# Gate modulation products of two blocks in one chained run, with four raw weight tiles and two tiles for each weight part

## The chip, the cores and the metric

The kernel runs on one core of a Trainium2 chip. The time is that of the device in microseconds (us), the median of the runs shown; one further execution was taken by the hardware profiler, and everything said of single instructions comes from it. The engines are called PE (matrix products; PEld is its loading of weights), DVE (vector), ACT (scalar and activation), POOL and SP (which issues the transfers).

## The reference

One step of a hybrid backbone: 128 context tokens and 512 latent tokens, model width 1024. Everything is float32.

```python
shift, scale, gate = jnp.split(mod, 3, axis=-1)      # mod = silu(c) @ w_ada + b_ada
h = _rmsnorm(x, g_pre) * (1 + scale) + shift
proj = h @ w_in                                      # 3840 columns
qa, ka, va, ga, qr, zf, zb, ir, gr, uf, gf = _split_columns(proj)
oa  = neighbourhood / context attention of (qa, ka, va)          # 8 heads x 64
o_r = bidirectional gated linear recurrence of (qr, zf, zb, ir)  # 4 heads, normed
o_f = Fourier mixing of uf, then a linear map
mixed = concat([oa * silu(ga), o_r * silu(gr), o_f * silu(gf)])
out = mixed @ w_out
x = x + gate * _rmsnorm(out, g_post)
```

The last third of `w_ada`, 1024 x 1024, makes `gate`, once for the context vector and once for the latent one. These products are what the change regroups.

## The kernel before

**Weights.** A block is 128 columns of `w_in` (BLOCKS, L24), a tile of 128 partitions by 1024 values, 512 KB. `load_raw` (L172) loads it into a tile tagged "raw"; all such loads are kept in program order on SP's queue. `split_w` (L178) makes two parts of it: `hi`, a rounded copy (a cast on ACT, L127), and `lo`, the remainder (a subtraction on DVE, L128). A product is three matmuls: hi with the high part of h, hi with its low part, lo with the high part (`mm3`, L208). The high and low parts of the modulated h stand in `hT[0]` and `hT[1]`. The dictionary WB (L27) says how many tiles a tag has: two "raw", three "hi", three "lo", eight "pT" of the same size, and so on. A tile is given again when all that read it is done, and whoever wants it waits until then.

**Start.** `start_stream` (L242) makes the modulated h in eight slices k = 0 to 7. For each slice `mod_cols` (L192) forms shift and scale for 128 columns with narrow matmuls: the stationary operand is 128 x 32 (`csil`), four of them side by side write four groups of 32 partitions, and each of the 8 float32 products becomes two instructions, so 16 for each block of 128 columns. Here two blocks (shift and scale) go into one PSUM tile one after the other. `zf_stream` (L281) follows slice by slice with the first two blocks, zf0 and zf1, whose parts are held until k = 7 is done: 2 blocks x 2 halves of the tokens x 8 slices x 3 matmuls of 320 columns. `fill` (L956) starts with "h4" and takes the other blocks in the order of FILL (L30); the first is zb0, whose first half goes along with the slices that are there. Two blocks of `ir` are held at once (`token_blocks`, L348).

**Middle.** The recurrence (L414) and the attention (L637) run beside the blocks as generators; a small planner, `Order` (L39), interleaves them in the program by estimated times. The tile framework then schedules the instructions with a timeline of its own, in which an instruction that is earlier in the program goes first when it is ready, and gives the tiles. What stands is an order for each engine that is fixed before the run.

**The gate.** `gate_vectors` (L844) waits for blocks WG = 18 onward. At each of eight blocks it loads 128 columns of `wg` into a "raw" tile, takes a PSUM tile with tag "f", runs `mod_cols` into it, and splits the 128 x 128 result into one half of two `row` tiles. After every second block, four matmuls with `selr` spread the rows over the partitions, and DVE adds the bias and multiplies by `g_post`. PSUM has eight tiles: five with tag "b", three with "f"; the accumulators of the blocks, the Fourier stage and the gate all use "f".

**End.** FILL ends with gf0, gf1, the two Fourier blocks uf0 and uf1, F0 (the Fourier stage joins the streams), ga2 and ga3. Then `out_first` (L895) computes the first 512 columns of the output projection and `out_second` (L919) the rest. `out_units` (L885) loads the four weight tiles kk in the order 2, 0, 1, 3 through "raw" and splits them into "hi" and "lo", or into two "pT" tiles for the kk that are named in `late`. The products run over k in the order 4, 5, 0, 1, 6, 7, 2, 3 (`kord`), where kk = k // 2, each in one accumulator; their moving operand is `w`, the stationary one `mh`, the split of the mixed branches.

`follow` (L115) is a helper that ties an instruction behind the last one of a list, as an order on the same engine; the recurrence and the attention scores use it.

Of the kernel before, what the change touches and what calls it, by code (L numbers as in the profile page):

```python
# [10 lines left out]
F32R = mybir.dt.float32r  # L11
# [6 lines left out]
P = 128  # L18
# [5 lines left out]
BLOCKS = ["zf0", "zf1", "zb0", "qr0", "zb1", "qr1", "ir0", "ir1", "gr0", "gr1", "va0", "qa0", "ka0", "ga0", "gf0", "va1",  # L24
          "qa1", "ka1", "ga1", "gf1", "va2", "qa2", "ka2", "ga2", "ga3", "va3", "qa3", "ka3", "uf0", "uf1"]
TOKENS = ("ir",)
WB = {"raw": 2, "hi": 3, "lo": 3, "t": 18, "pe": 2, "o": 4, "cf": 3, "pb": 5, "pf": 3, "s": 8, "m": 4, "row": 2, "tbl": 1, "pT": 8, "vs": 2, "kc": 4}  # L27
RAW = ["vs", "pT", "pT", "pT"] * 4
EARLY = 3
FILL = "zb0 qr0 zb1 qr1 ir0 P0 P1 ga0 P2 gr0 gr1 ga1 P3 gf0 gf1 uf0 F0 ga2 ga3"  # L30
# [41 lines left out]
def mixer_kernel(ctx: ExitStack, tc: tile.TileContext, A, O):  # L72
# [5 lines left out]
    wp = ctx.enter_context(tc.tile_pool(name="wp", bufs=1))  # L78
    tp = ctx.enter_context(tc.tile_pool(name="tp", bufs=WB["t"]))
    sp = ctx.enter_context(tc.tile_pool(name="sp", bufs=WB["s"]))  # L80
    ps = ctx.enter_context(tc.tile_pool(name="ps", bufs=8, space=PSUM))

    od = Order()
# [3 lines left out]
    def nm(s):  # L87
        n_[0] += 1
        return f"{s}_{n_[0]}"

    def T(cols=NT, dt=F32, tag=""):
        return tp.tile([P, NT], dt, tag="t", name=nm("t" + tag))[:, :cols]

    def PE_():
        return tp.tile([P, 512], F32, tag="pe", name=nm("pe"), bufs=WB["pe"])

    def S(cols):
        if cols <= 16:
            return sp.tile([P, 16], F32, tag="s", name=nm("s"))[:, :cols]
        return sp.tile([P, 320], F32, tag="m", name=nm("m"), bufs=WB["m"])[:, :cols]  # L100

    def C():
        return sp.tile([P, 256], F32, tag="cf", name=nm("cf"), bufs=WB["cf"])

    def PB(tag="b"):
        return ps.tile([P, 512], F32, tag=tag, name=nm("pb"), bufs=WB["p" + tag])

    last_tr = [None]

    def mm(out, lhsT, rhs, start=True, stop=True):  # L110
        n, m = rhs.free_size(), lhsT.free_size()
        od.now += 1e-3 * (n * 0.4167 * 4 if rhs.dtype == F32 else max(n * 0.4167, m * 0.83)) + 2e-3
        return te.matmul(out, lhsT, rhs, start=start, stop=stop).ins  # L113

    def follow(chain, ins):  # L115

        if chain:
            tc.add_manual_dep(ins, chain[-1].name, mybir.DependencyInfo(mybir.DependencyClass.NoSync,
                                                                        mybir.DependencyReason.DATA), reason="turns")
        chain.append(ins)  # L120
# [5 lines left out]
    def split(src, hi, lo, hi_eng=None, lo_eng=None):  # L126
        (sc.copy if hi_eng is None else hi_eng.tensor_copy)(hi, src)  # L127
        (ve if lo_eng is None else lo_eng).tensor_sub(lo, src, hi.bitcast(F32))  # L128
# [5 lines left out]
    def const(name, shape, dt=F32, dma=gp.dma_start):  # L134
        t = cp.tile([P, *shape], dt, tag=name, name=name)
        if name in A:
            dma(t, A[name])
        return t
# [27 lines left out]
    csil = const("csil", [KT, 32])  # L166
# [5 lines left out]
    def load_raw(src, tag, shape=(KT, P)):  # L172
        t = (tp if tag == "vs" else wp).tile([P, *shape], F32, tag=tag, name=nm(tag), bufs=WB[tag])
        with tc.issue_after(wdma[-1]) if wdma else ExitStack():
            wdma.append(sy.dma_start(t, src).ins)
        return t
# [6 lines left out]
    def load_w(src, lo_eng=None, shape=(KT, P), tags=("raw", "hi", "lo")):  # L183

        return split_w(load_raw(src, tags[0], shape), lo_eng, shape, tags[1:])

    def load(t, src):

        with tc.issue_after(wdma[-1]) if wdma else ExitStack():
            sy.dma_start(t, src)  # L190

    def mod_cols(out, w):  # L192

        t = od.now
        for k in range(KT):
            o = out[32 * (k % 4):32 * (k % 4) + 32, :]
            mm(o, csil[:, k, :], w[:, k, :], start=(k < 4), stop=(k >= 4))
        od.now = t + 0.45

    shift, G, rstd = const("shift", [KT, 2]), const("G", [KT, 2]), const("rstd", [5])  # L200
# [643 lines left out]
    def gate_vectors():  # L844
        selr = cp.tile([P, 2, P], F32R, tag="selr", name="selr")
        gp.tensor_copy(selr, sel)
        for q in range(8):
            yield f"block{WG + q}"
            hf = q // 4
            w = load_raw(A["wg"][q], "raw")  # L850
            if q % 4 == 0:
                gbias = T(512), T(512)
                for t, name in zip(gbias, ("bgate", "gpost")):
                    load(t, A[name][hf * 512:hf * 512 + 512].partition_broadcast(P))
                if True:
                    if q == 0:
                        gc = sp.tile([P, 2, 512], F32, tag="masks", name="gc", bufs=1)
                    gg[0][hf], gg[1][hf] = gc[:, hf, :], T(512)
                else:
                    gg[0][hf], gg[1][hf] = T(512), T(512)  # L860
            if q % 2 == 0:
                rows = [sp.tile([P, 256], F32R, tag="AC", name=nm("row"), bufs=2) for _ in range(2)]
            pm, es = PB("f"), slice(q % 2 * P, q % 2 * P + P)
            mod_cols(pm[:, 0:P], w)
            split(pm[:, 0:P], *[t[:, es] for t in rows])
            if q % 2 == 0:
                continue
            yield 1.0
            pg, cs = PB("f"), slice(q % 4 * P - P, q % 4 * P + P)
            for d in range(2):  # L870
                for a in range(2):
                    mm(pg[:, d * 256:d * 256 + 256], selr[:, d, :], rows[a], start=(a == 0), stop=(a == 1))
            for d in range(2):
                g = gg[d][hf][:, cs]
                ve.tensor_add(g, pg[:, d * 256:d * 256 + 256], gbias[0][:, cs])
                ve.tensor_mul(g, g, gbias[1][:, cs])
# [4 lines left out]
    def out_mm(po, w, i, k, first, last):  # L881
        for a, (pw, hh) in enumerate(((0, 0), (0, 1), (1, 0))):
            mm(po, mh[k][hh][:, i * P:(i + 1) * P], w[pw], start=(first and a == 0), stop=(last and a == 2))

    def out_units(hf, late):  # L885
        units = {}
        for kk in (2, 0, 1, 3):
            w = load_w(A["wout"][hf, kk], shape=(2, 512), tags=("raw", "pT", "pT") if kk in late else ("raw", "hi", "lo"))
            for j in range(2):
                units[2 * kk + j] = (w[0][:, j, :], w[1][:, j, :])  # L890
        return units
# [3 lines left out]
    def out_first():  # L895
        for k in kord[:2]:
            t = tp.tile([P, 2, NT], F32R, tag="vs", name=nm("mh"), bufs=WB["vs"])
            mh[k] = [t[:, j, :] for j in range(2)]
        mh[kord[2]] = [tp.tile([P, NT], F32R, tag="o", name=nm("mh"), bufs=WB["o"]) for _ in range(2)]
        rest = [big.tile([P, KT, NT], F32R, tag=f"hT{j}", name=f"mh{j}") for j in range(2)]  # L900
        for k in kord[3:]:
            mh[k] = [t[:, k, :] for t in rest]
        units = out_units(0, (3,))
        banks = [PB() for _ in range(4)]
        for n, k in enumerate(kord):
            yield f"m{k}"
            split(mx[k], *mh[k])
            yield 1.8
            for i in range(4):
                out_mm(banks[i], units[k], i, k, n == 0, n == KT - 1)  # L910
                yield 0
        banks.append(PB("b" if WB["pb"] > 4 else "f"))
        for n, k in enumerate(kord):
            out_mm(banks[4], units[k], 4, k, n == 0, n == KT - 1)
        for i in range(5):
            pos[i][0] = banks[i]
        yield 0
# [38 lines left out]
    def fill():  # L956
        yield "h4"
        for step in FILL.split():
            if step == "|":
                yield 0  # L960
                continue
            n, p = step[:2], int(step[-1])
            if n == "zb":
                yield from block(step, lambda z, u: gate(p, 1, z, u), ve)
            elif n == "qr":
                yield from block(step, lambda z, u: query(p, z, u), ve)
            elif n == "ir":
                yield from value_blocks()
            elif n[0] == "P":
                yield from attention_blocks(p)  # L970
            elif n[0] == "m":
                yield step
            elif n == "uf":
                yield from fourier_blocks()
            elif n == "F0":
                od.streams.insert(0, [fourier(), od.now])
            else:
                yield from gate_block(step)
        yield from out_first()
        yield from out_second()  # L980
# [7 lines left out]
    od.add(recurrence(1))  # L988
    od.add(attentions())
    od.add(gate_vectors())  # L990
    od.add(fill())
    od.run()
# [136 lines left out]
```

## Time and profile before

| | us |
|---|---|
| median of 3 runs | 436.22 (436.12 to 437.0) |
| profiled execution | 437.11 |
| its span | 435.3 |
| PE busy | 411.3 (94% of the span) |
| PE weight loads busy | 372.7 |
| DVE busy | 303.5 |
| ACT busy | 205.8 |

The span runs from the first instruction to the last. Busy times of PE are modelled from pipelined instructions, so that two that overlap both show their full duration; what one costs is read from the distance to the start of the next. Rows of the timeline give start, duration, engine, line, operation, the names of what is written and read, and how often it follows itself. A bracket at a row's end gives the idle time ahead of it and what ended it. A line is often that of a helper (L113 is every matmul, L127 and L128 every split), so the names of the tiles tell what it is: `raw,csil` are the gate's narrow matmuls, `hT,hi` and `hT,lo` those of the blocks, `hi,hT` those of ir, `hi,mh` and `pT,mh` those of the output projection, `t,t` those of the recurrence and of the Fourier stage.

### The profile page before, as it was taken

How to read it: one execution, taken by the hardware profiler on the slowest of the kernel's cores; microseconds unless marked ns; L12 is line 12 of the kernel's file. 1: busy time of each engine (PE TensorE's matmuls, PEld its weight loads, DVE VectorE, ACT ScalarE, POOL GpSimd, SP SyncE). 2: the span in 40 equal slices, each digit the busy share in tenths (PEclk: the TensorE clock that was granted, in tenths of full speed). 3: DMA queues.
4: the chain of work that ended last, by engine and by line, in shares of the span. 5: the costliest groups of instructions: out<-in, count | busy, mean ns of one | idle time of the engine just before them, and what ended most of it. 6: DMA issues, size and time to landing. Idle time of an engine off the chain costs nothing.

```text
span 435.3 us, 8309 instructions
## 1 busy us (share of the span) xinstructions
PE 411.3 (94%) x3176; PEld 372.7 (86%) x3176; DVE 303.5 (70%) x866; ACT 205.8 (47%) x546; POOL 7.4 (2%) x23
## 2 busy tenths in 40 slices
PE   0699999999998999999999999999999999999994
PEld 0488899999988998999899889889898988988884
DVE  2775479999986866885597658885768928670174
ACT  6434467565341526654444444753556643350161
POOL 2000000000020100000000000000000000000000
PEclk9999999999999999999999999999999999999998
DMA  7996153211302021122021413245134302481023
GB/s 236 412 407 229 49 158 114 74 45 50 88 20 76 10 62 48 56 97 74 32 68 60 145 50 104 98 147 163 51 119 150 96 0 66 140 291 48 0 105 139
DMA packets 19528, 47.62 MB, mean 109 GB/s; under 512 B 3184, under 2 KB 6912, under 8 KB 19488
## 3 DMA queue, kind: packets, MB, share of 16 engines
q1 hardware_dynamic: 19376, 46.94, 32.0%
q8 instruction: 25, 0.41, 0.4%
q0 software_dynamic: 112, 0.14, 0.3%
q14 instruction: 15, 0.12, 0.1%
HBM read 43.80 MB, written 3.28 MB: 108 GB/s over the span
## 4 chain that ended last, share of the span: by engine, by line
PE 90%; DVE 3%; DMA 3%; ACT 1%; issue 1%; SPq 0%; DVEq 0%; ACTq 0%
PE pb L113 84%; PE pb L124 7%; DMA vs<-wss 2%; DMA txa<-x 1%; DVE AL L450 1%; DVE t L524 1%; DVE AL L487 0%; ACT L679 0%; DVE t L951 0%; ACT pe L680 0%; DVE t L467 0%; DVE t L466 0%; DVE AC L450 0%; DVE t L468 0%; SPq L190 0%
## 5 line engine op out<-in xcount | busy, mean ns | idle before, releaser
L113 PE MATMUL pb<-hT,hi 128*128 128x320 f32 x896 | 208.7, 317 | 2.5 <-DVE vs L128 1.5
L113 PEld LDWEIGHTS pb<-hT,hi 128*128 128x128 f32 x896 | 148.7, 188 | 9.0 <-issue 3.3
L113 PE MATMUL pb<-hT,lo 128*128 128x320 f32 x448 | 139.1, 312 | 0.0
L113 PEld LDWEIGHTS pb<-hT,lo 128*128 128x128 f32 x448 | 84.0, 188 | 1.3 <-DVE G L272 0.2
L128 DVE TENSOR_TENSOR lo<-raw,hi 128x1024 fp32r<-128x1024 f32 x35 | 42.8, 1223 | 18.7 <-ACT hi L127 18.5
L127 ACT CAST hi<-raw 128x1024 fp32r<-128x1024 f32 x35 | 36.8, 1050 | 28.4 <-PE pb L113 17.5
L113 PE MATMUL pb<-t,t 64*128 64x128 f32 (+2 forms) x414 | 42.9, 291 | 0.4 <-DVE AL L450 0.4
L113 PEld LDWEIGHTS pb<-t,t 64*128 64x128 f32 (+1 forms) x414 | 36.0, 188 | 4.7 <-issue 0.7
L127 ACT CAST pT<-pb 128x256 fp32r<-128x256 f32 x64 | 23.5, 373 | 22.3 <-DVE pT L128 11.1
L113 PE MATMUL pb<-hi,mh 128*128 128x512 f32 (+1 forms) x108 | 30.8, 375 | 0.0
L128 DVE TENSOR_TENSOR pT<-pb,pT 128x256 fp32r<-128x256 f32 x64 | 26.5, 419 | 1.7 <-ACT pT L127 1.5
L679 ACT ACTIVATE pe<-pb,s 128x256 f32<-128x256 f32 x32 | 15.3, 478 | 17.5 <-DVE s L678 8.4
L113 PEld LDWEIGHTS pb<-hi,mh 128*128 128x128 f32 x108 | 19.6, 188 | 3.7 <-DVE mh L128 0.3
L113 PE MATMUL pb<-pT,mh 128*128 128x512 f32 (+1 forms) x102 | 21.9, 364 | 0.0
L124 PE MATMUL pb<-ident,pe 128*128 128x128 f32 x136 | 21.0, 274 | 0.5 <-ACT pe L680 0.5
L113 PEld LDWEIGHTS pb<-pT,mh 128*128 128x128 f32 x102 | 17.7, 189 | 3.1
L113 PE MATMUL pb<-lo,mh 128*128 128x512 f32 (+1 forms) x54 | 19.5, 375 | 0.0
L934 ACT ACTIVATE t<-pb 128x512 f32<-128x512 f32 (+1 forms) x11 | 6.1, 552 | 26.9 <-PE pb L113 26.7
L690 DVE TENSOR_TENSOR o<-pb,o 64x512 f32<-64x512 f32 (+1 forms) x16 | 7.8, 486 | 15.5 <-ACT o L689 15.4
L124 PEld LDWEIGHTS pb<-ident,pe 128*128 128x128 f32 x136 | 16.5, 140 | 1.7 <-ACT pe L680 0.7
L450 DVE COPY_PREDICATED AL<-masks,pb 128x512 f32<-128x512 uint32 x24 | 16.6, 742 | 1.7 <-PE pb L113 1.6
L113 PE MATMUL pb<-pT,vs 128*128 128x256 f32 (+1 forms) x96 | 17.0, 320 | 0.0
(205 smaller groups left out, 635.3 us busy)
## 6 DMA issues: line engine op xcount, KB each, us to landing
raw<-win SPq DMA_DIRECT2D x30, 512.0 KB, 3.5
pT<-wss SPq DMA_DIRECT2D x12, 512.0 KB, 10.3
raw<-wg SPq DMA_DIRECT2D x8, 512.0 KB, 3.6
raw<-wout SPq DMA_DIRECT2D x8, 512.0 KB, 3.6
t<-x SPq DMA_DIRECT2D x10, 256.0 KB, 5.4
o_y<-t SPq DMA_DIRECT2D x9, 256.0 KB, 2.2
vs<-wss SPq DMA_DIRECT2D x4, 512.0 KB, 9.5
tbl<-tbl SPq DMA_DIRECT2D x4, 512.0 KB, 3.5
```

Of the source, the lines that this page charges most:

```text
L113: return te.matmul(out, lhsT, rhs, start=start, stop=stop).ins
L124: last_tr[0] = te.transpose(out, src, ident).ins
L127: (sc.copy if hi_eng is None else hi_eng.tensor_copy)(hi, src)
L128: (ve if lo_eng is None else lo_eng).tensor_sub(lo, src, hi.bitcast(F32))
L450: ve.copy_predicated(out, mk.to_broadcast([P, i1 - i0, P]), src)
L524: ve.scalar_tensor_tensor(sall[r, cdst], sall[r, cs], Td[r, ip:ip + 1], pst[r, cdst], op0=ALU.mult, op1=ALU.add)
L679: sc.activation(pe[:, 256:512], ss[:, 256:512], ACT.Exp, bias=m[:, 1:2], accum_out=m[:, 3:4])
L690: ve.tensor_add(out, src[r, :], out)
L934: sc.activation(T(512)[:, cs], po[:, 0:cs.stop - cs.start], ACT.Square, accum_out=ssb[:, j:j + 1])
```

## The change

`mod_cols` ties its instructions behind one another through a list that the caller can hand on. `gate_vectors` loads nothing at an even block; at the odd one it loads both weights, runs the 32 instructions of the two in one chain into one PSUM tile of 256 columns, and splits 256 columns at once. The tag "raw" has four tiles, "hi" and "lo" two each. Since `out_units` has two pairs of "hi" and "lo", kk = 1 of the first half goes to "pT" along with kk = 3.

```diff
-WB = {"raw": 2, "hi": 3, "lo": 3, "t": 18, ...
+WB = {"raw": 4, "hi": 2, "lo": 2, "t": 18, ...
...
-    def mod_cols(out, w):
-
-        t = od.now
+    def mod_cols(out, w, chain=None):
+
+        t, chain = od.now, [] if chain is None else chain
         for k in range(KT):
             o = out[32 * (k % 4):32 * (k % 4) + 32, :]
-            mm(o, csil[:, k, :], w[:, k, :], start=(k < 4), stop=(k >= 4))
+            follow(chain, mm(o, csil[:, k, :], w[:, k, :], start=(k < 4), stop=(k >= 4)))
         od.now = t + 0.45
...
         for q in range(8):
             yield f"block{WG + q}"
             hf = q // 4
-            w = load_raw(A["wg"][q], "raw")
+            chain = []
             if q % 4 == 0:
...
             if q % 2 == 0:
-                rows = [sp.tile([P, 256], F32R, tag="AC", name=nm("row"), bufs=2) for _ in range(2)]
-            pm, es = PB("f"), slice(q % 2 * P, q % 2 * P + P)
-            mod_cols(pm[:, 0:P], w)
-            split(pm[:, 0:P], *[t[:, es] for t in rows])
-            if q % 2 == 0:
                 continue
+
+            rows = [sp.tile([P, 256], F32R, tag="AC", name=nm("row"), bufs=2) for _ in range(2)]
+            pm = PB("f")
+            for u, ww in enumerate([load_raw(A["wg"][q - 1 + j], "raw") for j in range(2)]):
+                mod_cols(pm[:, u * P:(u + 1) * P], ww, chain)
+            split(pm[:, 0:256], *rows)
             yield 1.0
...
-        units = out_units(0, (3,))
+        units = out_units(0, (1, 3))
```

`mod_cols` of the start stage is called without a chain, so that each of its calls ties its own 16 instructions.

More of the change, by code (lines that the diff above doesn't have):

```diff
@@ L26 @@
 TOKENS = ("ir",)
-WB = {"raw": 2, "hi": 3, "lo": 3, "t": 18, "pe": 2, "o": 4, "cf": 3, "pb": 5, "pf": 3, "s": 8, "m": 4, "row": 2, "tbl": 1, "pT": 8, "vs": 2, "kc": 4}
+WB = {"raw": 4, "hi": 2, "lo": 2, "t": 18, "pe": 2, "o": 4, "cf": 3, "pb": 5, "pf": 3, "s": 8, "m": 4, "row": 2, "tbl": 1, "pT": 8, "vs": 2, "kc": 4}
 RAW = ["vs", "pT", "pT", "pT"] * 4
```

## The prediction

> **What bounds the kernel now.** I read the page first (busy shares, then the chain of work that ended last), then the stretches view, whose columns are stretch, length, and each engine's busy time with its count.
>
> ```profile
> span 435.3 us, 8309 instructions
> ...
> PE 411.3 (94%) x3176; PEld 372.7 (86%) x3176; DVE 303.5 (70%) x866; ACT 205.8 (47%) x546; POOL 7.4 (2%) x23
> ...
> PE 90%; DVE 3%; DMA 3%; ACT 1%; issue 1%; SPq 0%; DVEq 0%; ACTq 0%
> ```
> ```profile
> core 0: us, PE busy (x) PEld busy (x) DVE busy (x) ACT busy (x) POOL busy (x), PEclk, DMA share, GB/s
> 54.00:134.00 80.00, 78.17 (x678) 73.37 (x678) 73.87 (x179) 45.13 (x107) 2.42 (x6) 1.00 0.24 75
> 134.00:385.00 251.00, 250.53 (x1850) 230.03 (x1851) 177.90 (x546) 121.74 (x362) 1.91 (x6) 1.00 0.27 86
> ```
>
> The chain is 90% PE. PE rests 80.00-78.17 = 1.83 us between 54 and 134 and 0.47 in the 251 us after that. So two things count: work taken off PE is a gain almost one for one, and a hole opened in PE is a loss almost one for one, because no later rest exists to swallow it. A deeper prefetch of raw weights (four tiles for two) has no hole to close between 134 and 385. The change makes PE's work smaller (the gate's runs) and thins the cover that keeps PE fed (two slots for a weight's parts where three stood).
>
> **Part 1, the gate's runs.** One gate block issues 16 of the narrow 128x32 instructions, eight blocks 128. Rows of the timeline of PE (start, duration), and one piece of the chain in order of time:
>
> ```profile
> 34.26 1.01 PE pb L113 x32
> ```
> ```profile
> 245.25 0.42 PE L113 MATMUL pb<-raw,csil 128*32 128x128 f32 x6
> 245.60 0.66 PE L124 MATMUL pb<-ident,pe 128*128 128x128 f32 x4
> ...
> 270.51 0.31 PE L113 MATMUL pb<-hT,lo 128*128 128x320 f32 x1
> 270.75 0.64 PE L113 MATMUL pb<-raw,csil 128*32 128x128 f32 x16
> 271.33 0.56 PE L113 MATMUL pb<-hT,hi 128*128 128x320 f32 x2
> ...
> 330.10 0.64 PE L113 MATMUL pb<-raw,csil 128*32 128x128 f32 x14
> ```
> ```profile
> 53.90:57.60 3.70, 3.65 (x25) 3.65 (x26) 0.00 (x0) 1.00 0.17 24
> ```
>
> In the timeline, what PE pays is the distance to the next row's start. A run of 16 takes 271.33-270.75 = 0.58 us; the chain's piece of 32, from the first stage, has the same instructions of two blocks in 1.01. The difference, 0.43 for 16, is 0.027 us an instruction, which leaves 0.15 a run whatever its length. Entering costs more: 270.75-270.51 = 0.24, where a 320-column matmul otherwise takes 3.65/25 = 0.147 (last row, the stretches view of the matmuls on hT). I put leaving at 0.10, an estimate of the size of entering (0.09). A run's fixed price is 0.15+0.09+0.10 = 0.34 us. From the first row (245.25) to the last (330.10) the timeline has thirteen runs: the eight blocks are cut five times, as by the transposes at 245.60. The added chain orders the 32 instructions of a pair among themselves; it keeps no others out. Bounds: four clean runs, 9 x 0.34 = **-3.1 us**; ten runs, if cuts come per instruction, **-1.0**. I take seven: 6 x 0.34 = **-2.0**.
>
> The work around them, from the views of the tiles row and raw and the page's list of DMA issues:
>
> ```profile
> L127 ACT CAST row<-pb x8: 266/268/283, 246.9 to 332.5; 128x128 fp32r<-128x128 f32 x8
> L128 DVE TENSOR_TENSOR row<-pb,row x8: 280/287/292, 247.4 to 332.8; 128x128 fp32r<-128x128 f32 x8
> ```
> ```profile
> L175 SPq DMA_DIRECT2D raw<-wg x8: 327/328/372, 204.9 to 314.6; - x8
> ```
> ```profile
> raw<-wg SPq DMA_DIRECT2D x8, 512.0 KB, 3.6
> ```
>
> Eight evictions on each engine become four of twice the width: between nothing and half of 8 x 0.28, a gain of 1.1 us on ACT and on DVE, behind a PE without a rest, so nothing. The eight gate loads stay eight; the even one is issued at the odd one's turn, on SP behind the loads of one more block. The first now stands 40 us ahead of its matmuls and the last 15 (314.6 to 330.1): nothing, and one landing of 3.6 us were the lead all gone. Four raw tiles hold a pair and leave two to the blocks between.
>
> **Part 2, two slots, at the start.** Both zf blocks keep their slots until the last modulated tile, k = 7. Today zb0 takes the third; rows of ACT, of DVE, of the stretches view for matmuls on hT, and of PE:
>
> ```profile
> 42.29 1.04 ACT L127 CAST hi<-raw 128x1024 fp32r<-128x1024 f32 x1
> ...
> 51.84 1.28 ACT L323 ACT_TABLE_LOAD   x1 [2.22 <-PE pb L113]
> 53.13 0.44 ACT L323 ACTIVATE t<-pb 128x320 f32<-128x320 f32 x1
> ```
> ```profile
> 44.23 1.22 DVE L128 TENSOR_TENSOR lo<-raw,hi 128x1024 fp32r<-128x1024 f32 x1
> ...
> 50.18 0.83 DVE L239 TENSOR_TENSOR hT<-t,hT 128x640 fp32r<-128x640 f32 x1
> ```
> ```profile
> 22.00:53.90 31.90, 20.52 (x120) 17.78 (x120) 10.02 (x15) 1.00 0.60 231
> ```
> ```profile
> 53.95 0.56 PE L113 MATMUL pb<-hT,hi 128*128 128x320 f32 x2 [1.02 <-ACT t L324]
> ```
>
> 120 matmuls on hT ran by 53.9; zf owns 2x2x8x3 = 96, so 24 are zb0's first half: 24 x 0.147 = 3.5 us that fill PE while it waits for k = 6 and 7. They can't run there any more. In return the subtraction at 44.23 (1.22 us) leaves DVE and those 24 leave PE's queue ahead of k = 7, whose tile I therefore put at 49.6 instead of 51.0. zf's first block then ends its 6 matmuls at 50.3; cast (1.04), subtraction (1.22) and two handovers of 0.1, an estimate, make zb0 ready at 52.8. If ACT takes the table load and a sigmoid first, as at 51.84 now, it is 1.7 later. PE then owes 46 matmuls where it owes 24 at 53.95 today: the loss is that time + 22 x 0.147 - 53.95, so 2.1 to 3.8, and 1.4 if k = 7 gains another 0.7. I take **+2.8**, the table load half avoided. Nothing else fills the hole: all other work needs zf, or a block behind zb0 in the same slots.
>
> **Middle.** A block lasts 48 x 0.147 = 7 us and its parts are ready some 2.5 us after a slot comes free, so one block ahead is enough, save for ir, which holds two pairs at once:
>
> ```profile
> 82.41 1.05 ACT L127 CAST hi<-raw 128x1024 fp32r<-128x1024 f32 x1 [1.98 <-PE pb L113]
> ...
> 101.77 1.05 ACT L127 CAST hi<-raw 128x1024 fp32r<-128x1024 f32 x1
> ```
> ```profile
> 83.84 1.39 PE L113 MATMUL pb<-t,t 64*128 64x128 f32 x20
> 85.15 0.50 PE L113 MATMUL pb<-hi,hT 128*128 128x256 f32 x2
> ...
> 104.38 0.45 PE L113 MATMUL pb<-hT,hi 128*128 128x320 f32 x2
> ```
>
> These casts run as qr1's slot and ir's first come free; after the change they serve ir's second part and va0, ready 2.5 us on, at 84.9 and 104.3. PE wants them at 85.15 (the recurrence's 20 run before) and 104.38. Nothing to 1.5 us: **+0.2**.
>
> **End.** In each accumulator the output projection's unit kk = 2 comes first. Today its cast takes the third slot at 341.26; rows of ACT and DVE, then the stretches view for matmuls on mh (the projection's) and for those on hT:
>
> ```profile
> 341.26 1.04 ACT L127 CAST hi<-raw 128x1024 fp32r<-128x1024 f32 x1 [0.17 <-PE pb L113]
> ...
> 364.83 1.05 ACT L127 CAST hi<-raw 128x1024 fp32r<-128x1024 f32 x1
> ```
> ```profile
> 367.66 1.22 DVE L128 TENSOR_TENSOR lo<-raw,hi 128x1024 fp32r<-128x1024 f32 x1
> ```
> ```profile
> 357.30:361.00 3.70, 2.20 (x9) 1.57 (x9) 0.00 (x0) 0.00 (x0) 1.00 0.00 0
> 364.70:373.30 8.60, 8.32 (x35) 6.32 (x35) 0.82 (x1) 0.07 (x1) 1.00 0.22 63
> ```
> ```profile
> 344.30:348.00 3.70, 3.65 (x24) 3.52 (x24) 0.00 (x0) 1.00 0.51 148
> 348.00:361.00 13.00, 0.12 (x1) 0.18 (x1) 0.00 (x0) 1.00 0.00 0
> 361.00:364.80 3.80, 3.75 (x24) 3.42 (x24) 0.00 (x0) 1.00 0.53 172
> ```
>
> The two hT rows with 24 are ga2's halves. With two slots ga2 and ga3 hold both, and kk = 2 waits for ga2's end at 364.8: the cast at 364.83 becomes its own, the subtraction ends at 368.9 (as now, behind Fourier's additions) or at 367.1 (DVE free at once). Gone are the 9 matmuls before 361, 2.1 us, and those from 365.2 until then: 1.9 to 3.7 us of hole. If the Fourier matmuls behind the 9 move up, they take the first 2.1 back. So 1.9 to 5.8; I take **+3.7**, moved up and DVE as busy as now. kk = 1 in pT costs the same cast and subtraction; kk = 0 waits for kk = 2's release, covered by ga3's 48 matmuls (7 us), and by nothing if ga3 runs early (2.5).
>
> **Sum.** -2.0+2.8+0.2+3.7 = +4.7 us. The profiled execution took 437.11 (its span 435.3, 1.8 around it), so 441.8; it stood 0.9 above the median of 436.22, on which it is **440.9**. The terms' ends: -3.1+1.4+0+1.9 = +0.2 (436.4) and -1.0+3.8+1.5+5.8 = +10.1 (446.3).
>
> **Rivals.**
> *Two slots are enough (faster).* PE's order is planned anew. If ga2's second 24 matmuls follow its first at 348 instead of 361, the slot is free 13 us sooner and kk = 2 is ready in time; the point that decides is ga2 ending 2.5 us before 357.3. Then the end costs nothing, and with the start at 1.4 and clean runs at -3.1 the sum is -1.7: 434.5 (433.1 with no hole at the start). For it: one block's length separates them, and nothing they multiply is late. Against it: PE passed them over for 13 us while it took the lower-ranked projection, so a PSUM bank held them, and that stays. [...]
> *The hole slows the clock (slower).* The stretches view at the end of the span, after PE's last matmul:
>
> ```profile
> 429.50:431.50 2.00, 0.00 (x0) 0.00 (x0) 1.54 (x4) 0.69 (x3) 0.00 (x0) 1.00 0.00 0
> 431.50:433.50 2.00, 0.00 (x0) 0.00 (x0) 0.50 (x2) 0.00 (x0) 0.00 (x0) 0.57 0.72 254
> ```
>
> The granted clock falls some 2 us after PE stops. [...] Against: the hole may be split in two. [...]
> *The runs stay cut (slower).* Twelve in place of thirteen: -0.3, and the sum is +6.4: 442.6. For it: five cuts in eight short groups.
>
> **Chances.** Forecast 0.55, enough slots 0.21, clock 0.12, cut runs 0.12. About 0.2% (0.9 us) is what a measurement here can tell from no change; the forecast's low end and weaker forms of the first rival give 0.08 to that: slower 0.73, same 0.08, faster 0.19. The range for 8 in 10 is 434.2 to 445.5; the forecast's own is 436.4 to 446.3.
>
> **What would show it.** About seven narrow runs after 240 us; zb0's cast behind zf's last matmul and a rest of PE of 2 us or more near 51; the projection's first matmul behind ga2's last, with rests near 357 or 365; PE's rests up by some 6 us. No rest near 365, or ga2's matmuls in one piece, would make it wrong.

## The result and the profile after

| | before | after |
|---|---|---|
| median, us (runs) | 436.31 (436.12 to 437.0, 4 runs) | 443.59 (443.14 to 443.88, 4 runs) |
| profiled execution, us | 437.11 | 443.88 |
| its span, us | 435.3 | 442.1 |

The ratio is 1.0163 with a 95% interval of 1.0145 to 1.0181: slower by 7.3 us, where the forecast had 4.7 us. An execution over 1.5% above the fastest of its kernel counts as slow and is in no median, interval or ratio of this document; that concerns two of four of the pairing alone and one of four of kk = 2 elsewhere. First the page of the profile after: the span, part 1 and the chain of work that ended last.

```profile
span 442.1 us, 8316 instructions
...
PE 413.4 (93%) x3176; PEld 374.5 (85%) x3176; DVE 303.5 (69%) x862; ACT 203.6 (46%) x542; POOL 7.4 (2%) x23
...
PE 86%; DVE 5%; DMA 4%; ACT 3%; issue 1%; SPq 1%; DVEq 0%; ACTq 0%
```

PE fell from 90% of the chain to 86%, and DVE, DMA and ACT rose: work that had been beside PE stands on the path now. The stretches view of the same two stretches that the prediction shows (columns as there) says where.

```profile
54.00:134.00 80.00, 79.62 (x673) 75.29 (x673) 69.30 (x164) 41.34 (x101) 2.42 (x6) 0.98 0.23 78
134.00:385.00 251.00, 247.38 (x1840) 227.40 (x1839) 180.65 (x556) 121.00 (x359) 1.91 (x6) 1.00 0.29 94
```

PE's rest between 134 and 385 us went from 0.47 to 251 - 247.38 = 3.62 us. In the first stretch PE looks busier than before, yet its granted clock is 0.98: part of that busy time is work at a clock of 0.50 (the rows below).

To see where the time went I lined the two traces up by PE's work: both lists of matmuls, each kind at the mean distance to its successor in the trace of before, and at each sum the time of after less the time of before.

| at (us of before) | 20 | 60 | 134 | 240 | 260 | 340 | 350 | 360 | 400 | 425 |
|---|---|---|---|---|---|---|---|---|---|---|
| after stands later by, us | -0.6 | 4.1 | 4.2 | 4.1 | 2.8 | 4.1 | 4.8 | 5.8 | 6.7 | 6.7 |

Its first value is a start that differs from run to run (the other traces here have -1.5 to 0). Other ways of pricing the kinds move single values by some tenths, so that little is not read. So the start stage cost 4.1 + 0.6 = 4.6 us (unrounded 4.05 + 0.58), the middle nothing, the gate's stage (240 to 340) nothing on balance, and the end 6.74 - 4.12 = 2.6 us. The dip at 260 is a gate run that came later than before, so that its work is still owed there.

**The start.** The timeline of after, one fence for each of DVE, PE and ACT; a bracket is the idle time ahead and what ended it.

```profile
48.19 0.83 DVE L239 TENSOR_TENSOR hT<-t,hT 128x640 fp32r<-128x640 f32 x1
52.73 1.23 DVE L128 TENSOR_TENSOR lo<-raw,hi 128x1024 fp32r<-128x1024 f32 x1 [3.72 <-ACT hi L127]
```
```profile
48.21 1.27 PE L113 MATMUL pb<-hT,hi 128*128 128x320 f32 x5 [1.08 <-DVE hT L238]
...
50.20 0.31 PE L113 MATMUL pb<-hT,lo 128*128 128x320 f32 x1
52.75 1.15 PE L113 MATMUL pb<-hT,hi 128*128 128x320 f32 x4 [2.25 <-ACT hi L127]
...
54.45 0.74 PE L113 MATMUL pb<-hT,hi 128*128 128x320 f32 x2
54.98 0.47 PE L113 MATMUL pb<-hT,lo 128*128 128x320 f32 x1
```
```profile
49.71 1.28 ACT L323 ACT_TABLE_LOAD   x1 [2.08 <-PE pb L113]
51.00 0.44 ACT L323 ACTIVATE t<-pb 128x320 f32<-128x320 f32 x1
51.34 0.43 ACT L324 ACTIVATE t<-pb 128x320 f32<-128x320 f32 x1
51.66 1.05 ACT L127 CAST hi<-raw 128x1024 fp32r<-128x1024 f32 x1
```

PE waits for zb0's cast, as forecast, and that cast stands behind a table load and two sigmoids. Then comes what the forecast gave only as a rival. The rows at 54.45 and 54.98 are 0.53 us apart for two matmuls: 0.27 each, where one takes 0.147 elsewhere. The stretches view of the same trace shows the granted clock in its third column from the end:

```profile
52.00:53.00 1.00, 0.25 (x1) 0.25 (x2) 0.27 (x1) 1.00 (x3) 0.00 (x0) 1.00 0.02 8
53.00:54.00 1.00, 0.90 (x4) 0.50 (x3) 1.00 (x2) 1.00 (x5) 0.00 (x0) 0.56 0.00 0
54.00:55.00 1.00, 0.99 (x4) 0.99 (x5) 1.00 (x3) 1.00 (x3) 0.00 (x0) 0.50 0.04 16
55.00:56.00 1.00, 1.00 (x5) 1.00 (x5) 1.00 (x2) 0.62 (x2) 0.00 (x0) 0.50 0.87 279
56.00:57.00 1.00, 1.00 (x6) 1.00 (x6) 1.00 (x3) 0.00 (x0) 0.00 (x0) 0.73 0.57 229
```

The clock lost is 0.44 + 0.50 + 0.50 + 0.27 = 1.7 us of full-speed work, just when zb0's matmuls have come. It is no accident of the profiled execution: the mean granted clock of all four executions of after is 0.992 to 0.993, where those of the kernel before beside the experiments have 0.995 to 0.999.

**The gate.** One pair in PE's timeline:

```profile
260.90 0.86 PE L113 MATMUL pb<-raw,csil 128*32 128x128 f32 x22
261.69 0.38 PE L113 MATMUL pb<-kc,tqs 64*128 64x256 f32 x1
262.00 0.62 PE L113 MATMUL pb<-raw,csil 128*32 128x128 f32 x10
```

An attention score goes in behind the 22nd of the 32. The four pairs have twelve runs, where before had thirteen. From the start of each run to PE's next other instruction, the twelve take 6.1 us and the thirteen 6.0.

**The end.** All rests over 0.2 us of PE between 345 and 375 us, and ACT's cast of kk = 2:

```profile
349.07 0.49 PE L113 MATMUL pb<-pT,vs 128*128 128x512 f32 x1 [0.29 <-ACT pT L127]
...
362.34 2.99 PE L113 MATMUL pb<-t,t 128*128 128x512 f32 x12 [0.88 <-ACT t L806]
...
370.06 2.59 PE L113 MATMUL pb<-hi,mh 128*128 128x512 f32 x10 [0.42 <-ACT hi L127]
```
```profile
368.96 1.04 ACT L127 CAST hi<-raw 128x1024 fp32r<-128x1024 f32 x1 [1.97 <-PE pb L113]
```

The projection's first matmul moved from 357.4 to 370.06, behind the cast that waited for ga2's last matmul. PE filled most of that time with other work and rested 1.6 us in three pieces. Only the last of them is the wait for this cast.

### The profile page after: what moved, and what is told of

It is laid out like the page before. It is cut to its first block, busy times and chain, and to the rows that moved or that the text cites. A ratio compares the mean times of both kernels' runs of the same rounds, so it can differ in the third digit from the quotient of the medians.

```text
span 442.1 us, 8316 instructions
## 1 busy us (share of the span) xinstructions
PE 413.4 (93%) x3176; PEld 374.5 (85%) x3176; DVE 303.5 (69%) x862; ACT 203.6 (46%) x542; POOL 7.4 (2%) x23
## 4 chain that ended last, share of the span: by engine, by line
PE 86%; DVE 5%; DMA 4%; ACT 3%; issue 1%; SPq 1%; DVEq 0%; ACTq 0%
PE pb L113 80%; PE pb L124 6%; DMA raw<-win 2%; DMA txa<-x 1%; ACT hi L127 1%; DMA raw<-wout 1%; DVE lo L128 1%; DVE AL L450 1%; DVE t L524 1%; SPq L190 0%; DVE AL L487 0%; ACT L679 0%; DVE pT L128 0%; DVE t L952 0%; ACT pT L127 0%
## 5 line engine op out<-in xcount | busy, mean ns | idle before, releaser
L128 DVE TENSOR_TENSOR lo<-raw,hi 128x1024 fp32r<-128x1024 f32 x34 | 41.6, 1223 | 27.2 <-ACT hi L127 26.9
L127 ACT CAST hi<-raw 128x1024 fp32r<-128x1024 f32 x34 | 35.6, 1051 | 39.2 <-PE pb L113 33.8
L113 PE MATMUL pb<-pT,mh 128*128 128x512 f32 (+1 forms) x132 | 28.7, 370 | 0.0
L113 PEld LDWEIGHTS pb<-pT,mh 128*128 128x128 f32 x132 | 23.4, 188 | 4.3
L113 PE MATMUL pb<-hi,mh 128*128 128x512 f32 (+1 forms) x88 | 24.0, 372 | 0.4 <-ACT hi L127 0.4
L113 PEld LDWEIGHTS pb<-hi,mh 128*128 128x128 f32 x88 | 15.9, 188 | 3.4 <-ACT hi L127 0.6
L113 PE MATMUL pb<-vs,csil 128*32 128x128 f32 x64 | 3.0, 313 | 14.4 <-DMA vs<-wss 14.4
L680 ACT ACTIVATE pe<-m,s 128x256 f32<-128x256 f32 x32 | 16.2, 505 | 0.0
```

The costliest lines, as they stand in the source:

```text
L680: sc.activation(pe[:, 0:256], sb, ACT.Exp, bias=m[:, 1:2], accum_out=m[:, 2:3])
```

## The experiments

My theory after the result: the time is lost by the two slots alone, at zb0 (a hole, then half clock) and at kk = 2; the pairing gives nothing because the runs stay cut. The rivals: pairing does gain and a further loss hides it; the clock is a symptom of no weight; kk = 2 costs all of the end.

### The slots alone

The kernel before with the buffers of after; the gate goes block by block.

```diff
-WB = {"raw": 2, "hi": 3, "lo": 3, ...
+WB = {"raw": 4, "hi": 2, "lo": 2, ...
...
-        units = out_units(0, (3,))
+        units = out_units(0, (1, 3))
```

> The gate is as before (one block at a time, no chain); raw has 4 tiles, hi and lo have 2, kk = 1 goes to pT. Theory (the slots cost it all): PE stands still behind zf's last matmul near 50 us and before the projection's first near 370, the clock falls after the first hole, and the time is that of the whole change, 443 to 444 us. Rival (pairing the gate's blocks costs it): 436 to 438 us.

Measured: 444.18 us, ratio 1.018 (1.0164 to 1.0195), against 1.0163 (1.0145 to 1.0181) of the whole change. A rest of 2.2 us for zb0's cast is there, and a granted clock of 0.50 from 53 to 55 us. So the slots cost the whole loss; the 0.6 us between the two medians are within the intervals, so pairing in this frame shows no gain. Unpaired, this kernel has eleven narrow runs, one fewer than the pairs.

### The pairing alone

Two raw tiles and three of each part, as before, with the gate of after. No kernel here has more than two raw tiles beside three of each part. The diff is against the kernel after.

```diff
-WB = {"raw": 4, "hi": 2, "lo": 2, ...
+WB = {"raw": 2, "hi": 3, "lo": 3, ...
-        units = out_units(0, (1, 3))
+        units = out_units(0, (3,))
```

> The gate's blocks are paired and chained, with the tiles of before (raw 2, hi and lo 3, kk = 3 alone in pT). Theory (the slots cost it all, and the runs stay cut): 436 +- 1 us, with 11 to 13 narrow runs after 240 us. Rival (pairing costs it): 440 us or more. The forecast's own term (seven runs): 434.3 us.

Measured: 443.29 and 448.02 us, ratio 1.0211 (1.0147 to 1.0275), slower than before in either. A miss, and ten narrow runs where 11 to 13 were expected. The profiled execution is the one of 443.29; the view of waits says for what PE rested (us in total, times, longest), and SP's timeline why.

```profile
PE pb L113 <- ACT hi L127: 4.0, 3, 1.4
PE pb L113 <- DVE lo L128: 1.5, 2, 0.8
```
```profile
282.80 1.98 SPq L175 DMA_DIRECT2D raw<-win  x2
...
288.36 2.96 SPq L175 DMA_DIRECT2D raw<-wg  x2
```

Both raw tiles go to the gate's pair, the next block's weights are loaded only when the pair gives them back (from 282.80 on), and PE stood at 287.12 for 1.44 us waiting for their cast. Lined up as above, this kernel is 0.6 us ahead of before at 240 us and 5.8 behind at 340. That is not all that it can cost: the mean granted clock was 0.996 in this execution and 0.984 in the other, and two more, of 450.18 and 452.59 us, had 0.985 and 0.978. At 448.02 us, 0.012 less clock is some 5 us of full-speed work, as much as the two times differ by; where in the kernel it was lost is not on record. So the pairing needs the deeper raw buffer, which I had priced at nothing in the prediction because no hole was there to close: right for the kernel before, but the change itself would have opened holes there.

### zb0's parts elsewhere

The change, with zb0's parts in two "pT" tiles, of which there are eight.

```diff
-        w = load_w(A["win"][BLOCKS.index(name)], lo_eng)
+        w = load_w(A["win"][BLOCKS.index(name)], lo_eng, tags=("raw", "pT", "pT") if name == "zb0" else ("raw", "hi", "lo"))
```

> The whole change, but zb0's two parts lie in pT tiles, which are free by then, so that its split does not wait for zf. Theory (start hole and the halved clock behind it cost 4.7 us): 438.9 us, 24 hT matmuls of zb0 before zf's end, granted clock 1.00 from 53 to 56 us. Rival (the start costs the forecast's 2.8): 440.8 us.

Measured: 438.42 us, 5.2 less than after; ratio 1.0058 (1.0038 to 1.0078). Its stretches view has PE waiting at 52 as before did, but at full clock:

```profile
52.00:53.00 1.00, 0.07 (x1) 0.07 (x1) 0.00 (x0) 0.99 (x4) 0.00 (x0) 1.00 0.00 0
53.00:54.00 1.00, 1.00 (x7) 1.00 (x8) 0.15 (x1) 1.00 (x2) 0.00 (x0) 1.00 0.03 8
54.00:55.00 1.00, 1.00 (x9) 1.00 (x8) 1.00 (x2) 1.00 (x5) 0.00 (x0) 1.00 0.00 0
```

The whole start cost is gone, hole and clock together; this run doesn't tell the two apart.

### The hole filled with idle work

The change, with 15 more matmuls behind zf's last whose result nobody reads. zb0 comes no sooner, but PE doesn't stand still.

```diff
...
+        idle = PB()
+        with tc.issue_after(end):            # end: zf's last matmul
+            for _ in range(15):
+                mm(idle[:, 0:320], hT[0][:, 7, 0:P], hT[0][:, 7, 0:320])
```

> The whole change, and 15 matmuls whose result nobody reads, put behind zf's last one, where PE otherwise waits for zb0's split. They do not bring zb0 forward; they only keep PE busy. Theory (1.5 us of the start's loss is the clock that falls after the rest): granted clock 1.00 from 53 to 57 us, and 442.1 us. Rival (the slow matmuls after the rest have another cause, late parts): 443.6 us or more.

Measured: 442.39 us, ratio 1.0126 (1.0113 to 1.0139), below the interval of after. The same hole in useful work, and the clock holds:

```profile
53.00:54.00 1.00, 0.95 (x7) 0.69 (x6) 0.49 (x1) 1.00 (x3) 0.00 (x0) 1.00 0.04 8
54.00:55.00 1.00, 0.59 (x4) 0.33 (x3) 1.00 (x2) 1.00 (x4) 0.00 (x0) 1.00 0.00 0
55.00:56.00 1.00, 1.00 (x8) 1.00 (x8) 1.00 (x3) 1.00 (x3) 0.00 (x0) 1.00 0.30 61
```

So the clock is a cost of its own beside the hole: 1.2 us by these times, 1.7 by the rows of after. The two nearly meet, for at full clock PE got through zb0's first matmuls on `hi` sooner and then rested for the low part, which after did not:

```profile
54.79 0.42 PE L113 MATMUL pb<-hT,lo 128*128 128x320 f32 x1 [0.41 <-DVE lo L128]
```

### kk = 2 elsewhere, alone and with zb0

```diff
-        units = out_units(0, (1, 3))
+        units = out_units(0, (2, 3))
```

> The whole change, but kk = 2 and 3 of the first half lie in pT, and kk = 0 and 1 take hi and lo, so that the projection's first unit does not wait for ga2. Theory (the end costs 2.6 us): 441.0 us, first matmul on mh near 362 us, before ga2's second half. Rival (the end costs the forecast's 3.7): 439.9 us. Rival (it costs nothing, the lag at the end is chance): 443.6 us.

Measured: 441.86 us (441.81 to 443.01), ratio 1.0132 (1.0115 to 1.015); only its times are read here. By the ratios 1.4 us came back and by the medians 1.7, with intervals that overlap, of the 2.6 us of the end.

> The whole change, with zb0's parts and kk = 2's in pT tiles. Theory (the two waits for a slot, and the halved clock behind the first, are all of the loss; pairing as such gives little, since the runs stay cut): the two gains of the single repairs, 5.2 and 1.2 us, add up, so 437.2 us. Rival (a third cost is hidden in the paired gate): 439 us or more. Forecast's term for the gate (-2.0 with no waits left): 434.3 us.

Measured: 437.2 us, ratio 1.0013 (1.0003 to 1.0022). Over zb0 alone, kk = 2 gives 1.2 us by the medians and 2.0 by the ratios. Lined up with before, this kernel is level from 20 to 340 us (-0.2 to -0.1), with twelve gate runs, and 0.6 to 0.8 behind from 360 on. So in a frame without either stall the pairing gains nothing, and some 0.7 us of the end is neither of the two slots; the only rest of PE that the view of waits names there is of 0.3 us, and where the remainder goes I leave open.

### The runs kept whole

The last kernel, with the pair's products raised in the scheduler's priority, so that nothing goes between them.

```diff
+            raws = [load_raw(A["wg"][q - 1 + j], "raw") for j in range(2)]
+            with tc.high_priority():
+                for u, ww in enumerate(raws):
+                    mod_cols(pm[:, u * P:(u + 1) * P], ww, chain)
```

> As both_in_pT, and the gate's narrow matmuls rank above all else in the scheduler, so that each pair's 32 stand together: 4 runs in place of 12. Theory (a run costs 0.34 us, and cuts are what ate the gate's gain): 8 x 0.34 = 2.7 us below both_in_pT, about 434.5 us. Rival (the run's price is hidden or the cuts cost nothing): within 0.5 us of both_in_pT.

Measured: 435.9 us, ratio 0.9981 (0.9969 to 0.9994), a miss by 1.4. PE's timeline has four such rows and no other narrow one:

```profile
250.32 1.08 PE L113 MATMUL pb<-raw,csil 128*32 128x128 f32 x32
...
322.29 1.08 PE L113 MATMUL pb<-raw,csil 128*32 128x128 f32 x32
```

Lined up with the kernel before it (both repairs, cut runs), it gains 4.1 us between 240 and 355 (some 3.5 of it by 340, where the gate's stage ends), more than the 2.7 that eight runs at 0.34 should give. The rows of the runs show 2.1 of it. Beside the runs of 22, 10, 16 and 32 shown so far, here is one of two, in after:

```profile
284.63 0.41 PE L113 MATMUL pb<-raw,csil 128*32 128x128 f32 x2
```

From a run's start to PE's next other instruction it is 0.34 us for 2, 0.55 for 10, 0.57 for 16, 0.79 for 22 and 1.01 for 32. In these rows the time goes up in steps of eight instructions and not by 0.027 us for each: the pair cut into 22 and 10 takes 0.79 + 0.55 = 1.34 us, the whole one 1.01. The twelve cut runs take 6.1 us, the four whole ones 4.0. The rest of the gain, at the runs' edges and in other work that the priority moves, is not told apart here.

Then it gives 2.7 back between 364 and 368. PE and DVE at that place:

```profile
365.23 2.94 PE L113 MATMUL pb<-t,t 128*128 128x128 f32 x24 [1.32 <-DVE tg L835]
```
```profile
363.77 1.21 DVE L128 TENSOR_TENSOR lo<-raw,hi 128x1024 fp32r<-128x1024 f32 x1
364.90 0.27 DVE L835 TENSOR_TENSOR tg<-pb,tg 128x128 f32<-128x128 f32 x1
```

The Fourier matmuls want a PSUM tile that L835 empties, and DVE had the subtraction of kk = 0 queued ahead of it: with PE earlier, DVE's fixed order is the bound there.

The same in the kernel before, each block's 16 instructions kept whole (eight runs for thirteen), with two raw tiles and three slots:

> The kernel before (blocks not paired, three slots), with its narrow gate matmuls ranked above all else: 8 runs in place of 13. Theory (0.34 us a run): 5 x 0.34 = 1.7 us below the kernel before, 434.6 us. Rival (no gain from whole runs, or the early rank makes other work late): 436.3 us or more.

Measured: 435.94 us, ratio 0.9983 (0.9974 to 0.9992). A miss in size: lined up with before it gains 0.8 us over the gate's stage, 0.16 a run, where the four pairs gave 3.5 / 8 = 0.4 a run over the same stage. By their rows the thirteen runs take 6.0 us and the eight 4.6, so 1.4 of own time went and not all of it arrived. The priority also moves other work, so these kernels don't give one price for a run; a fixed one such as my 0.34 misses that it depends on where the run is cut.

### The queue place at the end

Both repairs, the pairs kept whole, and GpSimd for that one subtraction of kk = 0.

```diff
-            w = load_w(A["wout"][hf, kk], shape=(2, 512), ...
+            w = load_w(A["wout"][hf, kk], gp if (hf, kk) == (0, 0) else None, shape=(2, 512), ...
```

> both_uncut with one edit more: GpSimd in place of VectorE takes the low part of Wout's block 0 for its first half of columns. In both_uncut that subtraction ran on DVE from 363.77 to 364.99 us ahead of the group that empties a Fourier PSUM tile, and TensorE rested 1.32 us at 365.23 for that tile. If that queue place is what gave the gain back, the rest goes and the time is 435.9 - 1.3 = 434.6 us. Rival: GpSimd's own subtraction takes longer than the way to the first projection matmul leaves, or the tile comes late for another reason; then a rest of a similar size stays near 365 us and the time is 435.5 to 436.5 us.

Measured: 435.23 us (434.71 to 435.39), ratio 0.9963 (0.9948 to 0.9977). POOL's subtraction, and PE where the rest was:

```profile
361.97 4.24 POOL L128 TENSOR_TENSOR lo<-raw,hi 128x1024 fp32r<-128x1024 f32 x1 [218.74 <-ACT hi L127]
```
```profile
363.71 1.20 PE L113 MATMUL pb<-pT,mh 128*128 128x512 f32 x4 [0.65 <-ACT mh L127]
364.75 3.51 PE L113 MATMUL pb<-t,t 128*128 128x128 f32 x30
```

The rest behind L835 is gone, so the queue place was its cause. Half of its worth arrived in the median (0.7 of 1.3 us), and the two intervals overlap, so the gain in time is not clear of noise: the rest just ahead of it, for the projection's `mh`, is 0.65 here and was 0.35. This version is 1.25 us faster than before and 8.4 faster than the change as made, the fastest of those run here.

## Why the prediction was right and where it was not

The forecast was 440.9 us and the measured time 443.59, within its range. The direction and the two places were right; the gate's gain did not come, and the start and the end were mis-sized.

**The start, +2.8: measured 4.6.** The hole itself was sized well, by luck, through errors that cancel. On before's scale of time the last modulated tile came at 49.02 + 0.58 = 49.6, as forecast. "The table load half avoided" failed: ACT took the load as the first block of zf ended (49.71), then two sigmoids, and the cast began 1.95 us later. But PE did not wait for the subtraction; the matmuls on `hi` began at the cast's end (52.75) and ran beside it. A handover, 0.1 us in the forecast as an estimate, was 0.02 us to DVE and 0.04 to PE (the cast ended at 52.71). And PE owed not 46 matmuls but all 48, for the 96 of zf were all that it had done on hT by then:

```profile
20.00:52.70 32.70, 17.43 (x96) 14.22 (x96) 10.53 (x16) 1.00 0.68 267
```

With 53.3 for 52.8 and 24 x 0.147 = 3.5 for 22 x 0.147, the forecast's own formula gives 53.3 + 3.5 - 53.95 = 2.9. The missing step was the clock, 1.7 us; the two make the 4.6.

**The clock rival**, with a chance of 0.12, was meant for the end hole. It came true at the start hole: I had thought of a rest as long as the end's term, 3.7 us, and passed over one of 2.2 at the start. How long a lower clock lasts ahead of more work no row of before shows; in after it was 3.4 us at 0.50, and 1.7 us of work lost. The end's clock stayed at 1.00; its hole was in three pieces, the longest of 0.88 us. Filling the start hole and giving zb0 its tiles both left the clock at 1.00 from 53 to 56 us.

**The gate, -2.0: measured 0.** The step that failed is "I take seven": twelve runs were left, the rival "the runs stay cut". The chain orders the 32 among themselves and does not keep an attention score out, which the prediction said and then discounted. The fixed price of a run failed too: the rows give 0.55 us for 10 instructions, 0.57 for 16 and 0.79 for 22. That cut runs cost time is shown: whole, they take 4.0 us of PE's time in place of 6.1, and that stage gained some 3.5 us.

**The rival "two slots are enough"** fell: PE passed ga2's second half over again, from 359.6 to 365.3, and the slot stayed taken.

**The middle, +0.2: measured 0.** PE waited for no block's parts there. But the deep raw buffer was not worth nothing: without it the pairing costs 5.8 + 0.6 = 6.4 us over the gate's stage.

**The end, +3.7: measured 2.6.** The mechanism held: ga2's last matmul, then the cast at 368.96, then the projection. Mis-sized was the cover. After the projection's first matmuls on `hi` the Fourier stage filled in:

```profile
372.49 1.95 PE L113 MATMUL pb<-t,t 128*128 128x128 f32 x16
374.19 1.17 PE L113 MATMUL pb<-lo,mh 128*128 128x512 f32 x4
```

The forecast let PE stand until the low part was there. Of the 2.6 us, the rests show 1.6, and the longest of them, 0.88 us, is no wait for a slot. PE waited for ACT's copy L806, which stood in ACT's order behind a cast that waited for a load of `wout`. Here is that cast in after, then in the kernel with zb0 in pT, whose order at the end is the same:

```profile
360.75 1.05 ACT L127 CAST pT<-raw 128x1024 fp32r<-128x1024 f32 x1 [1.58 <-DMA raw<-wout]
```
```profile
354.71 1.05 ACT L127 CAST pT<-raw 128x1024 fp32r<-128x1024 f32 x1 [0.67 <-DMA raw<-wout]
```

There the load came sooner relative to the work, PE has no such rest, and the end, lined up as above, costs some 1.5 us. Giving kk = 2 its own tiles returned 1.2 to 2.0, and the 0.7 that stayed then is not settled.

In sum 4.6 + 0 + 0 + 2.6 = 7.2 us, against 7.3 between the medians. That the total stayed in the range is in part luck: the start was 1.8 us and the gate 2.0 us worse than forecast, and the end 1.1 us better.

## What to carry to other kernels

Count a buffer's tiles where two are held at once, not over the mean of the stream: one place at the start and one at the end made two slots 7 us dearer than three, and moving two weights to tiles that were idle there took nearly all of it back (437.2 us). The order among the 32 instructions did not keep an attention score out from between them (in after it went in behind the 22nd); if a run is to stay whole, look in the planned order whether it does. And where a hole is opened ahead of dense matmul work, look at the granted clock behind it: here 1.7 us went to it behind a rest of 2.25 us.

## What the hardware showed

**Half clock came with rests of 2.25 and 2.2 us, and lasted 3.4 us.** From the means above, after ran at half clock for 0.88 + 1 + 1 + 0.54 = 3.4 us, from about 53.1; PE had rested for 2.25 us up to 52.75. The kernel with the slots alone has a rest of 2.2 us, ended at 53 - 0.29 = 52.71, and these rows:

```profile
52.00:53.00 1.00, 0.29 (x1) 0.29 (x2) 0.31 (x1) 1.00 (x3) 0.00 (x0) 0.76 0.02 8
53.00:54.00 1.00, 1.00 (x5) 0.77 (x4) 1.00 (x2) 1.00 (x4) 0.00 (x0) 0.50 0.00 0
54.00:55.00 1.00, 1.00 (x5) 1.00 (x5) 1.00 (x3) 1.00 (x2) 0.00 (x0) 0.50 0.24 16
55.00:56.00 1.00, 1.00 (x6) 1.00 (x6) 1.00 (x2) 0.58 (x2) 0.00 (x0) 0.54 0.74 233
```

That is 0.48 + 1 + 1 + 0.92 = 3.4 us again, from about 52.5. So the fall came some 0.4 us behind the end of the rest in after and, with the slots alone, 0.2 us ahead of it, some 2.0 us after PE had stopped.

Rests of 1.0 (before, at 53.95), 1.32 (the pairs kept whole, at 365.23) and 1.44 us (pairing alone, at 287.12) left the clock at 1.00 in the profiled executions. What decides between these rests and those of 2.2 is not shown.

**The gate's runs fell into four lengths.** Runs of 2 to 8 of the 128x32 instructions took 0.33 to 0.36 us, of 10 to 16 took 0.55 to 0.58, of 18 to 22 took 0.77 to 0.79 and of 32 took 1.01, over all the gate's runs in the traces above.

**The same subtraction** of 128 x 1024 took 4.24 us on POOL and 1.21 on DVE, where the profile's spans on POOL are rough.
